# Two half-step feed-forwards: first sums copied out ahead of weight blocks, and the last stream turned by VectorE and a DRAM tile

## The chip, the core and the metric

The kernel runs on one core of a Trainium2 chip. The metric is the device time of one execution in microseconds (us); the median of three runs of the kernel before is 977.78 us (977.39 to 977.93). The core has five engines that run their own queues of instructions and wait for each other by semaphores: TensorE (PE in the profile; its weight loads are listed apart as PEld), VectorE (DVE), ScalarE (ACT), GpSimd (POOL) and SyncE (SP). SP, ACT and POOL issue DMAs here.

## The reference

Two consecutive layers of a decoder trunk on 256 tokens of 1024 features, everything in float32, batch 1, with 256 memory tokens and a feed-forward width of 2816:

```python
def rmsnorm(x, g):
    y = x32 * lax.rsqrt(jnp.mean(x32 * x32, axis=-1, keepdims=True) + EPS)
    return y.astype(x.dtype) * g

def swiglu(x, w_gate, w_up, w_down):
    return (jax.nn.silu(x @ w_gate) * (x @ w_up)) @ w_down
...
    mem_n = rmsnorm(mem, mem_norm)
    for l in range(DEPTH):
        x = x + 0.5 * swiglu(rmsnorm(x, ffn1_norm[l]), ffn1_w_gate[l], ffn1_w_up[l], ffn1_w_down[l])
        h = rmsnorm(x, mix_norm[l])
...
        x = x + memory_cross_attention(rmsnorm(x, xa_norm[l]), mem_n, xa_w_q[l], xa_w_kv[l], xa_w_o[l])
        x = x + 0.5 * swiglu(rmsnorm(x, ffn2_norm[l]), ffn2_w_gate[l], ffn2_w_up[l], ffn2_w_down[l])
    return rmsnorm(x, final_norm)
```

In layer 0 the cut lines add a mixer of a short convolution and sliding-window attention, in layer 1 one of block-sparse attention. Each layer so has two half-step feed-forwards, ffn1 ahead of the mixer and ffn2 behind the memory attention.

## The kernel before

**Layout.** The stream `x` lies with features on the 128 partitions and tokens along the free axis: 8 tiles of 128x256, one per 128 features. A product contracts over features, so no transposes stand between the steps. Only the end is other: the last down projection writes tokens on partitions, so that the output leaves in its own layout, and for this the stream has to be turned once into `xtok`, 2 tiles of 128 tokens by 1024 features (it lies in the buffer named `bias`). `to_tokens` does this on TensorE: 16 transposes of 128x128 against `ident` (L469) into four tiles `tr`, each copied out by ScalarE as 128x512 (L470). `evac_tok` adds the last sums to `xtok`.

**Float32 by parts.** A float32 operand is split in a high part (type fp32r) and the rest. A weight tile of 128x128 times an `x` tile takes two matmuls: `whi` against both parts of x (L378, 512 columns) and `wlo` against the high part (L379, 256 columns). The two halves of the accumulator `acc` are then put together by `join`: ScalarE copies the one out (L388), VectorE adds the other (L389). There are four `acc` tiles.

**The weight stream.** All weights come in one list of 128x128 tiles in the order of use. SP loads chunks of 16 tiles (1 MB, `raw<-in_w`), up to three ahead. `Stream` splits them by blocks of 8 tiles: ScalarE copies the block to `whi` (L128), VectorE subtracts to get `wlo` (L129), 128x1024 each, with five buffers of each. `take` hands out tiles and marks blocks up to four ahead as due; a due block is split when somebody calls `fill` or `flush`, or at the latest when a tile of it is needed. `fine` makes the blocks come in two halves. `pin`, when set, holds the pieces of a block to the order in which the program writes them; without it the scheduler may move them ahead of other work. `memory` (the memory attention) sets `pin` at its start and clears it at its end.

**A feed-forward.** `ffn` runs over 22 tiles of the hidden width; for each there is a group for gate and one for up, in two parts of four weight tiles: eight tiles, one block, one accumulator each. The products are taken of x times the norm's gain alone; the scale by the root mean square comes later. `squares` sums the squares of the tiles, `norm_scale` puts sums (L347), the power on GpSimd (L351) and the spread over partitions (L357) among the matmuls, and sets `n.ready`. Groups that end before that are joined, and their `evac` (scale, silu, product, split into `h`) waits in `n.waiting`. `evac` and the down projections flush due blocks.

**What sets the order.** `Order.run` writes the groups in sequence and tasks between them by an estimated time (`pe.after(delay, fn, cost)`). A scheduler then orders each engine's queue by estimated times, except what is kept in program order. The eight tiles `x` of a new norm come out of the preceding projection one by one, so at the start of ffn2 the first groups' matmuls stand interleaved: each new tile is used for the groups that are open.

Of the kernel before, what the change touches and what calls it, by code (L numbers as in the profile page):

```python
# [15 lines left out]
F32 = mybir.dt.float32  # L16
F32R = mybir.dt.float32r
AF = mybir.ActivationFunctionType
# [5 lines left out]
P = 128  # L24
D = 1024
KT = D // P
S = 256
# [196 lines left out]
def halves(t):  # L224

    return t.rearrange("p (b a) -> p b a", b=2)
# [17 lines left out]
def build(nc, tc, ctx, a):  # L244
    consts = ctx.enter_context(tc.tile_pool(name="consts", bufs=1))
    wpool = ctx.enter_context(tc.tile_pool(name="wpool", bufs=1))
    act = ctx.enter_context(tc.tile_pool(name="act", bufs=1))
    psum = ctx.enter_context(tc.tile_pool(name="psum", bufs=1, space=PSUM))
    dram = ctx.enter_context(tc.tile_pool(name="dram", bufs=1, space=DRAM))

    def acc_tile():
        return psum.tile([P, 512], F32, name="acc", bufs=4)
# [4 lines left out]
    def tr_tile():  # L257
        return psum.tile([P, 512], F32, name="tr", bufs=2)

    def w1():  # L260
        return act.tile([P, S], F32, name="w1", bufs=8)
# [8 lines left out]
    x = consts.tile([P, KT, S], F32, name="x")  # L270
# [3 lines left out]
    ws = Stream(nc, wpool, a["w0"], a["w"])  # L274
# [4 lines left out]
    ident = consts.tile([P, P], F32, name="ident")  # L279
# [8 lines left out]
    pt = tr_tile()  # L288
# [3 lines left out]
    pe = Order()  # L292
# [45 lines left out]
            nc.scalar.activation(sq, stream[:, k], AF.Square)  # L338
            nc.vector.tensor_tensor(n.acc, n.acc, sq, op=ALU.add)

    def norm_scale(n, delay=2300):


        def sums():
            pt = tr_tile()
            for t in range(2):
                nc.tensor.matmul(pt[:, t:t + 1], n.acc[:, t * P:(t + 1) * P], ones, start=True, stop=True)  # L347
            ms = act.tile([P, 2], F32, name="ms", bufs=2)
            nc.vector.tensor_scalar(ms, pt[:, :2], 1.0 / D, EPS, op0=ALU.mult, op1=ALU.add)
            n.rcol = act.tile([P, 2], F32, name="rcolm" if n.keep else "rcol", bufs=1 if n.keep else 2)  # L350
            nc.gpsimd.tensor_tensor(n.rcol, ms, mhalf, op=ALU.pow)  # L351
            pe.after(2200, spread, 120)

        def spread():
            pt = tr_tile()
            for t in range(2):
                nc.tensor.transpose(pt[:, t * P:(t + 1) * P], n.rcol[:, t:t + 1].to_broadcast([P, P]), ident)  # L357
            n.rbc = act.tile([P, S], F32, name="rbcm" if n.keep else "rbc", bufs=1 if n.keep else 2)
            nc.scalar.activation(n.rbc, pt[:, :S], AF.Copy)
            n.ready = True  # L360
            ws.fine = False
            for fn in n.waiting:
                fn()
            n.waiting = []

        pe.after(delay, sums, 250)

    def when_scaled(n, fn):
        if n.ready:
            fn()  # L370
        else:
            n.waiting.append(fn)


    def mm(ps, w, x2, start, stop):


        nc.tensor.matmul(ps, w[0], x2.both, start=start, stop=False)  # L378
        nc.tensor.matmul(ps[:, :S], w[1], x2.high, start=False, stop=stop)  # L379
# [7 lines left out]
    def join(out, ps):  # L387
        nc.scalar.activation(halves(out), unpaired(ps[:, S:]), AF.Copy)  # L388
        nc.vector.tensor_tensor(halves(out), unpaired(ps[:, :S]), halves(out), op=ALU.add)  # L389
        return out  # L390
# [62 lines left out]
    def split_tile(src):  # L453
        return split_into(h_tile(), src)
# [6 lines left out]
            nc.vector.tensor_tensor(lo, src, hi.bitcast(F32), op=ALU.subtract)  # L461

    def to_tokens(out):
        def go():
            for u in range(2):
                for c in range(2):
                    pt = tr_tile()
                    for k in range(4):
                        nc.tensor.transpose(pt[:, k * P:(k + 1) * P], x[:, 4 * c + k, u * P:(u + 1) * P], ident)  # L469
                    nc.scalar.activation(out[:, u, c * 512:(c + 1) * 512], pt, AF.Copy)  # L470
        return go


    def ffn(which, layer, n, nxt, first=False, last=False):
# [14 lines left out]
        def gate_up(f, part, ks):  # L489
            def go():  # L490
                if ks[0] == 0:
                    cur[f, part] = acc_tile()
                ps = cur[f, part]
                w = f"{which}_w_{'up' if part else 'gate'}"
                for k in ks:
                    mm(ps, ws.take(w, layer, k * P, f * P), n.x[k], k == 0, k == KT - 1)
                if ks[-1] == KT - 1:
                    cur[f, part] = join(w1(), ps)
                    if part == 1:
                        when_scaled(n, lambda: evac(f, cur[f, 0], cur[f, 1]))  # L500

            return always, go, len(ks) * 327

        def evac(f, g, u):

            nc.vector.tensor_tensor(g, g, n.rbc, op=ALU.mult)
            nc.scalar.activation(g, g, AF.Silu)
            ws.fill()
            nc.vector.tensor_tensor(u, g, u, op=ALU.mult)
            ws.fill()  # L510
            h[f] = split_tile(halves(u))
            ws.flush()
# [73 lines left out]

        if first:
            pe.after(12000, lambda: [squares(n, k, x) for k in range(KT)], 0)
        norm_scale(n, 18200 if first else 2300)
        parts = (range(4), range(4, KT))  # L590
        ups = [(always, gates, FIRST * 327)] if first else []
        ups += [gate_up(f, part, ks) for f in range(FT) for part in range(2) for ks in parts
# [1 line left out]
        if last:  # L594
            xtok = act.tile([P, 2, D], F32, name="bias", bufs=1)
            gfin = act.tile([P, D], F32, name="kT", bufs=1)
            src = a["final_norm"]
            nc.sync.dma_start(gfin, bass.AP(tensor=src.tensor, offset=src.offset, ap=[[0, P], [1, D]]))
            pe.after(20000, to_tokens(xtok), 2000)
        pe.run(ups + (down_tok() if last else [down(j) for j in range(KT)]))  # L600


# [420 lines left out]
    def memory(layer, n, nxt, k2):  # L1023
        o = [None] * 4
        v2 = act.tile([P, 2, 2, 512], F32R, name="bias", bufs=1)

        def scale():
            n.rs = small("rs")
            nc.vector.tensor_scalar(n.rs, n.rcol, 128 ** -0.5, None, op0=ALU.mult)

        def evac_q(h):
            def fn(t):
                at = slice(h * P, (h + 1) * P)
                attend_all(n, split_into(q2_tile(), t), k2[h], lambda u: (v2[:, 0, u, at], v2[:, 1, u, at]),
                           lambda: made.get((layer, h // 2), math.inf), collector(o, h))
                ws.step()
            return fn

        when_scaled(n, scale)
        norm_scale(n)  # L1040
        ws.pin = tc.keep_in_program_order
        f = [group("xa_w_q", layer, h * P, n, evac_q(h), scaled=False) for h in range(4)]
        v = [mem_v_group(layer, i, v2[:, 0], v2[:, 1]) for i in range(2)]
        pe.run(f[0] + f[1] + v[0] + f[2] + f[3] + v[1] + out_proj("xa_w_o", layer, o, nxt, (2, 3)))
        ws.pin = None


    xn = lambda key: new_normed(key, "x", KT)
    n = xn(("ffn1_norm", 0))
# [50 lines left out]
    n, nxt = nxt, xn(("xa_norm", 0))  # L1100
    even_mixer(n, nxt, bias, sinks, kv2_tiles(), mem_keys(0))
    n, nxt = nxt, xn(("ffn2_norm", 0))
    memory(0, n, nxt, keys[0])
    bias = load_bias(1)
    n, nxt = nxt, xn(("ffn1_norm", 1))
    ffn("ffn2", 0, n, nxt)
    n, nxt = nxt, xn(("mix_norm", 1))
    ffn("ffn1", 1, n, nxt)
    n, nxt = nxt, xn(("xa_norm", 1))
    odd_mixer(n, nxt, bias, mem_keys(1))  # L1110
    n, nxt = nxt, xn(("ffn2_norm", 1))
# [74 lines left out]
```

## Time and profile before

| what | us |
|---|---|
| median of three runs | 977.78 |
| the profiled execution | 977.58 |
| its span | 975.8 |

How to read it: a timeline row has the start within the span, the duration, the engine, line and operation, output<-inputs, shapes, and in brackets a wait and what ended it. A waits row has the waiting instruction, the engine and line that ended the wait, then the total, the count and the mean in us. A group row ends with the total busy time, the mean in ns and the idle time before. The buffers' numbers are left out in the profile. The rows themselves stand in the prediction, where they are used.

### The profile page before, as it was taken

How to read it: one execution, taken by the hardware profiler on the slowest of the kernel's cores; microseconds unless marked ns; L12 is line 12 of the kernel's file. 1: busy time of each engine (PE TensorE's matmuls, PEld its weight loads, DVE VectorE, ACT ScalarE, POOL GpSimd, SP SyncE). 2: the span in 40 equal slices, each digit the busy share in tenths (PEclk: the TensorE clock that was granted, in tenths of full speed). 3: DMA queues.
4: the chain of work that ended last, by engine and by line, in shares of the span. 5: the costliest groups of instructions: out<-in, count | busy, mean ns of one | idle time of the engine just before them, and what ended most of it. 6: DMA issues, size and time to landing. Idle time of an engine off the chain costs nothing.

```text
span 975.8 us, 16900 instructions
## 1 busy us (share of the span) xinstructions
PE 963.8 (99%) x6576; PEld 903.5 (93%) x6576; DVE 759.2 (78%) x1355; ACT 614.1 (63%) x1139; POOL 27.7 (3%) x42
## 2 busy tenths in 40 slices
PE   8999999999999999999999999999999999999997
PEld 7899999999999899999999999999999989999896
DVE  7988777798878888876778888677877788888663
ACT  7666655696667666665556666556775767666541
POOL 1100000001000000000000000000000000000010
PEclk9999999999999999999999999999999999999999
DMA  9797556555535555656556566565645346565631
GB/s 354 292 352 258 180 210 206 173 186 197 189 131 210 189 210 213 198 195 212 193 196 203 192 211 205 187 213 173 241 148 195 102 158 225 206 210 186 210 130 43
DMA packets 28496, 194.73 MB, mean 200 GB/s; under 512 B 3298, under 2 KB 3938, under 8 KB 5760
## 3 DMA queue, kind: packets, MB, share of 16 engines
q1 hardware_dynamic: 27072, 187.84, 55.5%
q0 software_dynamic: 912, 5.37, 1.5%
q8 instruction: 51, 0.84, 0.3%
q10 hardware_dynamic: 432, 0.44, 0.1%
q14 instruction: 29, 0.24, 0.1%
HBM read 192.57 MB, written 4.22 MB: 202 GB/s over the span
## 4 chain that ended last, share of the span: by engine, by line
PE 97%; DVE 1%; DMA 0%; issue 0%; ACT 0%; SPq 0%; POOLq 0%
PE acc L378 41%; PE acc L379 21%; PE acc L383 7%; PE acc L385 7%; PE acc L384 7%; PE acc L555 1%; PE acc L554 1%; PE acc L553 1%; PE acc L891 1%; PE acc L890 1%; PE acc L892 1%; DMA raw<-in_w 0%; PE sc L553 0%; PE sc L555 0%; PE sc L554 0%; PE tr L687 0%
## 5 line engine op out<-in xcount | busy, mean ns | idle before, releaser
L128 ACT ACTIVATE whi<-raw 128x1024 fp32r<-128x1024 f32 (+2 forms) x375 | 369.8, 990 | 286.1 <-PE acc L378 141.4
L129 DVE TENSOR_TENSOR wlo<-raw,whi 128x1024 fp32r<-128x1024 f32 (+2 forms) x375 | 427.4, 1142 | 154.8 <-ACT whi L128 145.3
L378 PE MATMUL acc<-x,whi 128*128 128x512 f32 x1392 | 457.5, 383 | 3.5 <-DVE w L389 2.6
L379 PE MATMUL acc<-x,wlo 128*128 128x256 f32 x1392 | 377.6, 273 | 0.6 <-DVE wlo L129 0.6
L378 PEld LDWEIGHTS acc<-x,whi 128*128 128x128 f32 x1392 | 262.2, 189 | 40.4 <-DVE w L389 2.8
L379 PEld LDWEIGHTS acc<-x,wlo 128*128 128x128 f32 x1392 | 267.2, 192 | 1.7 <-DVE wlo L129 0.9
L378 PE MATMUL acc<-h,whi 128*128 128x512 f32 x462 | 151.3, 382 | 0.0
L379 PE MATMUL acc<-h,wlo 128*128 128x256 f32 x462 | 125.5, 273 | 0.0
L378 PEld LDWEIGHTS acc<-h,whi 128*128 128x128 f32 x462 | 87.1, 189 | 12.0
L379 PEld LDWEIGHTS acc<-h,wlo 128*128 128x128 f32 x462 | 88.7, 192 | 0.2
L384 PE MATMUL acc<-h,whi 128*128 128x256 f32 x322 | 87.8, 276 | 0.0
L385 PE MATMUL acc<-h,wlo 128*128 128x256 f32 x322 | 87.7, 275 | 0.0
L383 PE MATMUL acc<-h,whi 128*128 128x256 f32 x322 | 86.5, 276 | 0.0
L384 PE MATMUL acc<-x,whi 128*128 128x256 f32 x304 | 84.1, 278 | 0.0
L385 PE MATMUL acc<-x,wlo 128*128 128x256 f32 x304 | 83.8, 278 | 0.0
L383 PE MATMUL acc<-x,whi 128*128 128x256 f32 x304 | 83.0, 277 | 0.0
L389 DVE TENSOR_TENSOR w<-acc,w 128x256 f32<-128x256 f32 x195 | 81.4, 418 | 0.3
L388 ACT ACTIVATE w<-acc 128x256 f32<-128x256 f32 x195 | 72.0, 370 | 5.4 <-PE acc L379 5.2
L384 PEld LDWEIGHTS acc<-h,whi 128*128 128x128 f32 x322 | 61.7, 192 | 0.1
L385 PEld LDWEIGHTS acc<-h,wlo 128*128 128x128 f32 x322 | 61.7, 192 | 0.1
L383 PEld LDWEIGHTS acc<-h,whi 128*128 128x128 f32 x322 | 60.6, 192 | 0.4 <-DVE x L441 0.2
L384 PEld LDWEIGHTS acc<-x,whi 128*128 128x128 f32 x304 | 58.2, 192 | 0.2
(205 smaller groups left out, 1159.7 us busy)
## 6 DMA issues: line engine op xcount, KB each, us to landing
raw<-in_w SPq DMA_DIRECT2D x171, 1024.0 KB, 4.9
dists<-line POOLq DMA_DIRECT2D x2, 1536.0 KB, 12.2
raw<-in_memT SPq DMA_DIRECT2D x3, 1024.0 KB, 5.1
raw<-in_w SPq DMA_DIRECT2D x6, 384.0 KB, 6.1
bias<-dists POOLq DMA_DIRECT2D x2, 1024.0 KB, 11.4
x<-in_xT SPq DMA_DIRECT2D x1, 1024.0 KB, 7.6
out<-bias SPq DMA_DIRECT2D x2, 320.0 KB, 2.4
kT<-in_final_norm SPq DMA_DIRECT2D x1, 512.0 KB, 5.3
```

The costliest lines, as they stand in the source:

```text
L128: for ins in (self.nc.scalar.activation(hi[:, at], src, AF.Copy), self.nc.vector.tensor_tensor(lo[:, at], src, hi[:, at].bitcast(F32), op= ...
L129: self.nc.vector.tensor_tensor(lo[:, at], src, hi[:, at].bitcast(F32), op=ALU.subtract)):
L378: nc.tensor.matmul(ps, w[0], x2.both, start=start, stop=False)
L379: nc.tensor.matmul(ps[:, :S], w[1], x2.high, start=False, stop=stop)
L383: nc.tensor.matmul(ps[:, :S], w[0], x2.high, start=start, stop=False)
L384: nc.tensor.matmul(ps[:, :S], w[0], x2.low, start=False, stop=False)
L385: nc.tensor.matmul(ps[:, :S], w[1], x2.high, start=False, stop=stop)
L388: nc.scalar.activation(halves(out), unpaired(ps[:, S:]), AF.Copy)
L389: nc.vector.tensor_tensor(halves(out), unpaired(ps[:, :S]), halves(out), op=ALU.add)
L553: nc.tensor.matmul(ps, hh, wh, start=f == 0, stop=False)
L554: nc.tensor.matmul(ps, hh, wl, start=False, stop=False)
L555: nc.tensor.matmul(ps, hl, wh, start=False, stop=f == FT - 1)
```

## The change

Three edits. First, in ffn1 and ffn2 `gate_up` flushes the due blocks behind each join as long as the norm's scale isn't ready. Second, `pin` is no longer cleared at the end of `memory` but by `norm_scale` of the feed-forward behind it, once its scale is ready. So at the start of ffn2 the blocks are split in the program's order behind the joins, whereas the scheduler placed them before. Third, `to_tokens` no longer uses TensorE. For each pair of x tiles VectorE transposes 128x512 in squares of 32x32 into a tile `q2` (two buffers); eight GpSimd DMAs of 32x8x32 (runs of 32 elements) write it to a DRAM tile `tok`, 32 DMAs in all; one more loads `tok` into `xtok`. It starts 6000 (the order's estimated ns) behind the norm's scale in place of 20000 behind the start of the feed-forward, and its transposes and stores are kept in program order.

```diff
-    def norm_scale(n, delay=2300):
+    def norm_scale(n, delay=2300, unpin=False):
...
             n.ready = True
             ws.fine = False
+            if unpin:
+                ws.pin = None
...
     def to_tokens(out):
-        def go():
-            for u in range(2):
-                for c in range(2):
-                    pt = tr_tile()
-                    for k in range(4):
-                        nc.tensor.transpose(pt[:, k * P:(k + 1) * P], x[:, 4 * c + k, u * P:(u + 1) * P], ident)
-                    nc.scalar.activation(out[:, u, c * 512:(c + 1) * 512], pt, AF.Copy)
-        return go
+        tok = dram.tile([S, D], F32, name="tok")
+        to = tok.rearrange("(c i) (k p j) -> p k i c j", i=32, p=4, j=32)
+        for k in range(0, KT, 2):
+            t = act.tile([P, 2 * S], F32, name="q2", bufs=2)
+            tc.keep_in_program_order(nc.vector.transpose(t, x[:, k:k + 2].rearrange("p k s -> p (k s)")))
+            for p in range(4):
+                for i in range(2):
+                    tc.keep_in_program_order(nc.gpsimd.dma_start(
+                        to[p, k + i], t[32 * p:32 * p + 32, i * S:(i + 1) * S].rearrange("i (c j) -> i c j", j=32)))
+        nc.gpsimd.dma_start(out, tok.rearrange("(u q) f -> q u f", u=2))
...
                     if part == 1:
                         when_scaled(n, lambda: evac(f, cur[f, 0], cur[f, 1]))
+                    if not n.ready:
+                        ws.flush()
...
-        norm_scale(n, 18200 if first else 2300)
+        norm_scale(n, 18200 if first else 2300, unpin=True)
...
-            pe.after(20000, to_tokens(xtok), 2000)
+            when_scaled(n, lambda: pe.after(6000, lambda: to_tokens(xtok), 0))
...
         pe.run(f[0] + f[1] + v[0] + f[2] + f[3] + v[1] + out_proj("xa_w_o", layer, o, nxt, (2, 3)))
-        ws.pin = None
```

Below are queue rows with the buffers' numbers, which name a tile through the program. Lines of the changed kernel are higher by 2 at the matmuls and joins (L378 to L389 are L380 to L391), by 8 in `evac`.

ScalarE's queue at the start of ffn2 in layer 0, before (`x_4022` is the last x tile of this norm; `acc_4030`, `acc_4059`, `acc_4098` are the sums of groups 0 to 2, `whi_4086` and `whi_4091` the blocks of groups 4 and 5):

```order
L128 ACTIVATE whi_4086<-raw_3940 128x1024
L317 ACTIVATE x_4022<-x_69,vecs_70 128x2x128
L338 ACTIVATE sq_4025<-x_69 128x256
L128 ACTIVATE whi_4091<-raw_3940 128x1024
L388 ACTIVATE w1_4049<-acc_4030 128x256
L128 ACTIVATE whi_4142<-raw_4031 128x1024
L388 ACTIVATE w1_4076<-acc_4059 128x256
L128 ACTIVATE whi_4147<-raw_4031 128x1024
L388 ACTIVATE w1_4117<-acc_4098 128x256
```

The same place of ScalarE's queue in the changed kernel (groups 0 to 2 are `acc_4030`, `acc_4063`, `acc_4098`; the blocks of groups 4 and 5 are `whi_4052` and `whi_4083`):

```order
L317 ACTIVATE x_4022<-x_69,vecs_70 128x2x128
L338 ACTIVATE sq_4025<-x_69 128x256
L390 ACTIVATE w1_4049<-acc_4030 128x256
L128 ACTIVATE whi_4052<-raw_3940 128x1024
L390 ACTIVATE w1_4080<-acc_4063 128x256
L128 ACTIVATE whi_4083<-raw_3940 128x1024
L128 ACTIVATE whi_4142<-raw_4031 128x1024
L128 ACTIVATE whi_4147<-raw_4031 128x1024
L390 ACTIVATE w1_4117<-acc_4098 128x256
```

The copy of group 0 stood behind group 5's block and now stands ahead of group 4's; group 4's block has moved from ahead of the last x tile to behind that copy. VectorE's queue moves likewise.

TensorE's queue at the same start, before, from the end of group 3's (`acc_4120`) thirteen matmuls on (`acc_4154` is group 4):

```order
L378 MATMUL acc_4120<-x_3998,whi_4004 128x512
L379 MATMUL acc_4120<-x_3998,wlo_4005 128x256
L378 MATMUL acc_4030<-x_4022,whi_3884 128x512
L379 MATMUL acc_4030<-x_4022,wlo_3885 128x256
L378 MATMUL acc_4059<-x_4022,whi_3909 128x512
L379 MATMUL acc_4059<-x_4022,wlo_3910 128x256
L378 MATMUL acc_4098<-x_4022,whi_3958 128x512
L379 MATMUL acc_4098<-x_4022,wlo_3959 128x256
L378 MATMUL acc_4120<-x_4022,whi_4004 128x512
L379 MATMUL acc_4120<-x_4022,wlo_4005 128x256
L347 MATMUL tr_4052<-ones_95,sqacc_3982 128x1 x2
L378 MATMUL acc_4154<-x_3904,whi_4086 128x512
```

And in the changed kernel, from group 2's pair on the tile before the last:

```order
L380 MATMUL acc_4098<-x_3998,whi_3958 128x512
L381 MATMUL acc_4098<-x_3998,wlo_3959 128x256
L380 MATMUL acc_4030<-x_4022,whi_3884 128x512
L381 MATMUL acc_4030<-x_4022,wlo_3885 128x256
L380 MATMUL acc_4063<-x_4022,whi_3909 128x512
L381 MATMUL acc_4063<-x_4022,wlo_3910 128x256
L380 MATMUL acc_4098<-x_4022,whi_3958 128x512
L381 MATMUL acc_4098<-x_4022,wlo_3959 128x256
L381 MATMUL acc_4120<-x_3904,wlo_4005 128x256
L380 MATMUL acc_4120<-x_3917,whi_4004 128x512
L381 MATMUL acc_4120<-x_3917,wlo_4005 128x256
```

The last pairs of groups 0 to 2 stood behind thirteen matmuls of group 3 and now stand ahead of them, right behind group 2's pair on the tile before.

VectorE's queue in ffn2 of layer 1 in the changed kernel, at the third and fourth of the new transposes (`q2` is the transposed tile, `raw`, `whi` and `wlo` belong to weight blocks, `acc` to a join, `h` to the hidden tiles):

```order
L391 TENSOR_TENSOR w1_9920<-acc_9901,w1_9920 128x256
L472 STREAM_TRANSPOSE q2_9666<-x_69 128x512
L449 TENSOR_TENSOR h_9898<-w1_9884,h_9898 128x2x128
L514 TENSOR_TENSOR w1_9920<-w1_9920,rbc_9570 128x256
L129 TENSOR_TENSOR wlo_10002<-raw_9902,whi_10001 128x1024
L391 TENSOR_TENSOR w1_9940<-acc_9923,w1_9940 128x256
L517 TENSOR_TENSOR w1_9940<-w1_9920,w1_9940 128x256
L129 TENSOR_TENSOR wlo_10007<-raw_9902,whi_10006 128x1024
L391 TENSOR_TENSOR w1_9976<-acc_9957,w1_9976 128x256
L449 TENSOR_TENSOR h_9954<-w1_9940,h_9954 128x2x128
L472 STREAM_TRANSPOSE q2_9676<-x_69 128x512
```

The first two transposes stand together in front of the third of three L449 further up in this queue; the four are new, and the rows between them are those of before. On GpSimd's queue the 32 stores and the load stand behind the last L351 and ahead of the end's operations.

## The prediction

> **What bounds the kernel.** I read the busy times first, then the chain of waits, then the waits of TensorE by what ended them.
>
> ```profile
> span 975.8 us, 16900 instructions
> PE 963.8 (99%) x6576; PEld 903.5 (93%) x6576; DVE 759.2 (78%) x1355; ACT 614.1 (63%) x1139; POOL 27.7 (3%) x42
> PE 97%; DVE 1%; DMA 0%; issue 0%; ACT 0%; SPq 0%; POOLq 0%
> PE acc L378 <- DVE w L389: 2.6, 2, 1.3
> PE acc L378 <- ACT whi L128: 0.6, 1, 0.6
> PE acc L379 <- DVE wlo L129: 0.6, 1, 0.6
> ```
>
> TensorE (PE) is busy for 963.8 of 975.8 us and carries 97% of the chain. A change gains only by taking instructions off PE or by closing one of its waits. The largest waits (total, count, mean) are two, 2.6 us together, for the VectorE (DVE) half of a join. So the question is where these two stand, and how much PE work the change removes. The profiled execution took 977.58 us, 1.78 around its span; the median of the runs shown is 977.78, 0.20 above it.
>
> ```profile
> 322.39 0.38 PE L379 MATMUL acc<-x,wlo 128*128 128x256 f32 x2
> ...
> 324.58 0.38 PE L378 MATMUL acc<-x,whi 128*128 128x512 f32 x1
> 324.79 0.27 PE L379 MATMUL acc<-x,wlo 128*128 128x256 f32 x1
> ...
> 325.89 0.50 PE L347 MATMUL tr<-ones,sqacc 128*128 128x1 f32 x4
> ...
> 327.70 0.48 PE L378 MATMUL acc<-x,whi 128*128 128x512 f32 x1 [1.31 <-DVE w L389]
> ```
>
> ```profile
> 804.56 0.48 PE L378 MATMUL acc<-x,whi 128*128 128x512 f32 x1 [1.31 <-DVE w L389]
> ```
>
> The timeline of PE (start, duration, instruction, wait in brackets) shows the start of the second feed-forward in layer 0, and the same wait in layer 1. Four accumulators exist; the fifth group, the row at 327.70, needs that of group 0. PE stopped at 327.70 − 1.31 = 326.39. Group 0 got its last pair of matmuls only at 324.58 and 324.79 and closed about 325.0, because 13 matmuls of group 3 stand ahead of it in PE's order.
>
> ```profile
> 324.99 1.06 ACT L128 ACTIVATE whi<-raw 128x1024 fp32r<-128x1024 f32 x1 [4.63 <-PE acc L378]
> 325.96 0.37 ACT L388 ACTIVATE w<-acc 128x256 f32<-128x256 f32 x1
> ```
>
> ```profile
> 320.97 0.48 DVE L318 SCALAR_TENSOR_TENSOR x<-x,vecs 128x256 fp32r<-128x256 f32 x1
> ...
> 326.08 1.23 DVE L129 TENSOR_TENSOR wlo<-raw,whi 128x1024 fp32r<-128x1024 f32 x1 [3.16 <-PE acc L379]
> 327.23 0.42 DVE L389 TENSOR_TENSOR w<-acc,w 128x256 f32<-128x256 f32 x1
> ```
>
> The timelines of ScalarE (ACT) and DVE tell the other half. ACT idled 4.63 us in front of a weight block whose buffer group 0 still held, then split it for 1.06 us, and only then copied group 0 out (0.37). DVE stood likewise: 1.23 us of wlo, then the add of the join. From group 0's close to the join's end at 327.65 pass 2.65 us, 2.29 of them a weight block.
>
> **The two gaps: minus 2.62 us.** In the changed order ACT has the last x tile, its square, join 0, then the blocks; PE has the three last-tile pairs of groups 0 to 2 ahead of group 3's remainder. PE finished group 2's previous pair with the first of the two L379 at 322.39, about 322.6. The last x tile was there at 320.97 + 0.48 = 321.45, and it moves ahead of a 1.23 us wlo on DVE and a 1.06 us whi on ACT, so it is no later.
>
> ```profile
> 859.68 0.38 PE L378 MATMUL acc<-x,whi 128*128 128x512 f32 x1
> ...
> 862.30 0.38 PE L378 MATMUL acc<-x,whi 128*128 128x512 f32 x1
> ```
>
> These two rows are eight pairs apart, one group of steady work: 2.62 us, 0.327 a pair. Group 0 therefore closes near 322.6 + 0.33 = 322.9, 2.1 us earlier than before. The ACT copy takes 0.37 and the DVE add 0.42: done about 323.9 with 0.1 per hand-over, 2.5 us ahead of 326.39.
>
> What is late next? The block of group 4, split ahead of the last x tile before, now stands behind join 0. Its whi runs about 323.4 to 324.4 (1.06), its wlo 324.4 to 325.7 (1.23 and a hand-over). PE wants whi at 326.39 and wlo 0.2 later: a margin of **0.7 to 1.0 us**. The block of group 5 follows join 1, ends near 327.2 and is wanted at 326.39 + 2.62 = 329.0. Joins 2 and 3, behind three blocks, come near 330.0 and 331.6 on DVE; wanted at 326.39 + 2 × 2.62 = 331.6 and 334.3. Each has over 1.5 us. So both gaps close, 2 × 1.31 = 2.62. Bounds: nothing gained (rival 1), and no more than the 2.62 that the rows hold.
>
> The same edits touch the start of the first feed-forward of layer 1, near 497 us, where blocks now come in two halves behind the joins.
>
> ```profile
> 328.00:500.00 172.00, 172.00 (x1075) 158.86 (x1074) 133.39 (x216) 104.68 (x179) 2.11 (x2) 1.00 0.59 202
> ```
>
> This window (length, then busy PE, weight loads, DVE, ACT, POOL, clock, DMA share, GB/s) covers that start. PE is busy all 172.00 us, so there is nothing to gain; join 0 would wait behind two halves, some 2.4 us, and has 4 us before PE asks. I put it at nothing.
>
> **The 16 transposes: minus 1.50 us.** They stand among layer 1's gate and up groups, in the PE queue.
>
> ```profile
> 807.50 0.60 PE L469 MATMUL tr<-ident,x 128*128 128x128 f32 x4
> 807.85 0.46 PE L378 MATMUL acc<-x,whi 128*128 128x512 f32 x1
> ...
> 815.79 1.04 PE L469 MATMUL tr<-ident,x 128*128 128x128 f32 x8
> 816.59 0.46 PE L378 MATMUL acc<-x,whi 128*128 128x512 f32 x1
> ...
> 820.82 0.60 PE L469 MATMUL tr<-ident,x 128*128 128x128 f32 x4
> 821.17 0.36 PE L379 MATMUL acc<-x,wlo 128*128 128x256 f32 x1
> ```
>
> From start to start of the next matmul they hold PE for 0.35, 0.80 and 0.35 us: 1.50. The four ACT copies of L470 go too; ACT is 63% busy and no wait of PE names them: nothing.
>
> **What replaces them: nothing on the path, as long as GpSimd issues at its usual pace.** Four DVE transposes of 128x512 arrive, then 32 DMAs of 32 KB and one of 1 MB, all issued by GpSimd (POOL). The trace has no DVE transpose; the nearest rows of that shape are:
>
> ```profile
> L332 DVE TENSOR_TENSOR w<-w,w 128x512 f32<-128x512 f32 x18 | 12.3, 684 | 0.1
> L567 DVE CUSTOM_DVE_ANT_0 w<-bias 128x512 f32<-128x512 f32 x2 | 2.5, 1230 | 0.0
> ```
>
> So 0.68 to 1.23 us each, 2.7 to 4.9 in all; I take 0.68, the row with eighteen instances. What hides them is DVE's 22% of idle time and the distance between a group's close and the use of its accumulator: 3 × 2.62 = 7.86 us, less 0.8 for the join, or **about 6.5 us of cover** with hand-overs. Below nothing is excluded for DVE and POOL work, since neither takes anything off PE.
>
> The danger is a wait. The tile that a transpose writes has two buffers, so transpose 3 waits on DVE until the eight DMAs of transpose 1 have landed, transpose 4 for those of transpose 2, and behind each queue the wlo blocks and joins that PE needs.
>
> ```profile
> 816.77 1.09 DVE L447 TENSOR_TENSOR h<-w,h 128x256 fp32r<-128x256 f32 x3
> ...
> 832.92 0.41 DVE L447 TENSOR_TENSOR h<-w,h 128x256 fp32r<-128x256 f32 x1
> ...
> 838.16 0.42 DVE L447 TENSOR_TENSOR h<-w,h 128x256 fp32r<-128x256 f32 x1
> ```
>
> ```profile
> 307.72 0.98 POOL L845 DMA_DIRECT2D bias<-dists  x1 [26.53 <-PE tr L706]
> 307.00:318.00 11.00, 11.00 (x92) 10.75 (x92) 10.52 (x24) 8.99 (x19) 0.98 (x1) 1.00 0.77 286
> L845 POOL DMA_DIRECT2D bias<-dists x2 | 1.9, 948 | 34.0 <-PE tr L706 26.5 <-PE acc L379 7.5
> line<-kT POOLq DMA_DIRECT2D x1, 24.0 KB, 2.4
> bias<-in_onehot POOLq DMA_DIRECT2D x1, 99.0 KB, 6.9
> raw<-in_w SPq DMA_DIRECT2D x171, 1024.0 KB, 4.9
> ```
>
> The first fence is DVE's timeline; the second has a row of POOL's, the window around it, a group row (busy, mean ns) and DMA rows (size, us to landing).
>
> By the order, transposes 1 and 2 come in the run of three at 816.77, transpose 1 ending near 818.1; transpose 3 just before 832.92, transpose 4 just after 838.16, near 838.6. An issue takes i = 0.95 (the mean of 948 ns, two rows), and landing 2.4 to 6.9 (24 and 99 KB), say 4.6. Eight issues have landed 818.1 + 7.6 + 4.6 = 830.3, ahead of 832.9. Sixteen: 818.1 + 15.2 + 4.6 = 837.9, ahead of 838.6; with 6.9 it is 840.2, a wait of 1.6 under 6.5 of cover. Cost nothing. The 1 MB back load is issued about 846 (transpose 4's eight issues) and is first used after 940; at 4.9 us for such a load it has ample room. The 8192 runs of 128 B share the queues with the weight loads, which land in 4.9 us, come in chunks used in 2 × 2.62 = 5.24 us, and are asked for three chunks ahead: nothing.
>
> **Sum:** 977.58 − 2.62 − 1.50 = 973.46 for the profiled execution; 0.20 above it, as the median stands: **973.7 us**, 0.42% less.
>
> **A rule that speaks against it.** The issue at 307.72 took 0.98 us in a window where DVE was busy for 10.52 of 11 us, so it was held by at most a small part of DVE's work. The Trainium skill, page "SBUF — State Buffer", section "SBUF: two separate sides" (its box on the "DVE blocks DMA" trap and what follows it), says that a DMA issued from GpSimd can't write its descriptors while VectorE holds the shared port in a two-port operation, and gives about 620 ns alone against 3100 beside one. By an estimate from that page, i would be 3.1, and by rival 2 below the loss 16 × 3.1 + 4.6 − 27 = 27 us, the time about 1001. By this rule the issue at 307.72 should have been stretched too; its 0.98 us agrees with the page only if the DVE operations beside it were of another kind.
>
> **Rivals.**
>
> 1. *The gap moves to the next in line.* Where group 4's block stands behind join 0, a delay of 0.7 to 1.0 us in any of four hand-overs opens PE's wait again, now for wlo in place of the join. If it stays as long as it was, only the transposes are gained: 977.78 − 1.50 = **976.3**, within 0.2%. In part: near 975. For it: the margin is the smallest of the sum, and one hand-over is enough. Against: it starts 2.1 us earlier than before.
>
> 2. *Issues on GpSimd stretch, and DVE stands still behind the third and fourth transpose.* The point from which this decides: the loss is 16i + 4.6 − 20.5 − 6.5, with 20.5 = 838.6 − 818.1. It is nothing up to i = 1.40 and eats the whole gain of 4.12 at i = 1.66.
>
> ```profile
> 280.50 0.69 POOL L351 TENSOR_TENSOR rcol<-ms,mhalf 128x2 f32<-128x2 f32 x1 [40.85 <-DVE ms L349]
> 327.80 1.61 POOL L351 TENSOR_TENSOR rcol<-ms,mhalf 128x2 f32<-128x2 f32 x1 [19.11 <-DVE ms L349]
> ```
>
> That POOL does stretch is in these rows: one operation, 0.69 and 1.61 us. By this ratio i = 0.95 × 2.33 = 2.2, and the loss 35.2 + 4.6 − 27 = 12.8: 973.7 + 12.8 = **986.5**, slower. Against: both DMA issues of that kind took about 0.95, and those here have a thirty-second of the bytes.
>
> That the edits don't reach the order can be left out: the rows of the changed order show join 0 ahead of the blocks.
>
> **Chances.** Forecast 0.66. Rival 1: 0.20, of which 0.14 within 0.2% (975.8 to 979.7, about what a measurement of this kernel tells from no change) and 0.06 short of it. Rival 2: 0.14, slower. Faster 0.66 + 0.06 = 0.72, same 0.14, slower 0.14. The range goes from 972.6 (the sum and 1 us for what two rows of 0.6 and the run-to-run spread hold) to 976.4 (rival 1 in full), leaving out 0.14 for rival 2 and a few hundredths below.
>
> **What would show it.** Right: no wait of over 0.3 us on PE near 326 and 803, no transposes of x on PE, DVE transposes of 0.6 to 1.2 us, POOL's issues about 0.95 apart, no DVE wait of over 6 us near 832 and 838. Wrong: a PE wait for L129 or L128 at the fifth group (rival 1), or a DVE wait at the third or fourth transpose with a PE wait for a join behind it (rival 2).

## The result and the profile after

| | before | changed |
|---|---|---|
| median, us | 977.86 (977.39 to 977.93, 6 runs) | 972.52 (972.07 to 973.35, 6 runs) |
| the profiled execution / its span, us | 977.58 / 975.8 | 972.72 / 970.9 |

The ratio of the changed kernel to before is 0.9947, with a 95% interval of 0.9934 to 0.996: between 3.9 and 6.5 us faster, 5.2 at the middle. The forecast was 973.7 with 972.6 to 976.4: the median is 1.2 us under the forecast and 0.1 under the low end of the range. By the ratio, 0.9947 of the 977.78 that the forecast starts from, it is 972.6, just on that end. One execution of e1, one of e2 and one of the kernel before beside e9 and e10 took 1685 to 3594 us and are left out of the medians and ratios below.

First the busy times of the changed kernel, the share of the chain, and the waits of TensorE (total, count and longest; the third number is not the mean, as it is called above):

```profile
PE 961.6 (99%) x6560; PEld 901.4 (93%) x6560; DVE 761.1 (78%) x1361; ACT 612.7 (63%) x1137; POOL 47.5 (5%) x75
PE 98%; DVE 1%; DMA 0%; ACT 0%; SPq 0%; issue 0%; POOLq 0%
PE tr L290 <- DVE warm L273: 1.1, 1, 1.1
PE acc L380 <- ACT whi L128: 1.0, 1, 1.0
PE acc L381 <- DVE wlo L129: 0.6, 1, 0.6
PE acc L380 <- DVE x L318: 0.3, 1, 0.3
```

The 2.6 us for the join are gone. What is left are waits in the first 24 us of the span.

The timelines of ScalarE and VectorE, at the place that the prediction showed of before (line numbers are 2 higher now):

```profile
323.47 0.38 ACT L390 ACTIVATE w<-acc 128x256 f32<-128x256 f32 x1 [2.33 <-PE acc L381]
323.75 1.05 ACT L128 ACTIVATE whi<-raw 128x1024 fp32r<-128x1024 f32 x1
...
323.88 0.42 DVE L391 TENSOR_TENSOR w<-acc,w 128x256 f32<-128x256 f32 x1 [1.79 <-ACT w L390]
324.83 1.23 DVE L129 TENSOR_TENSOR wlo<-raw,whi 128x1024 fp32r<-128x1024 f32 x1 [0.52 <-ACT whi L128]
```

ScalarE now waits for group 0's last matmul in front of the copy, not in front of a block. Join 0 ends at 324.30, the block of group 4 at 326.06.

To see where the time went, the same matmuls are set side by side: the timeline of TensorE before (first fence) and changed (second), in each the second matmul of group 4 in layer 0, that of group 4 in layer 1, and one just behind the last transposes.

```profile
328.02 0.27 PE L379 MATMUL acc<-x,wlo 128*128 128x256 f32 x1
...
804.88 0.27 PE L379 MATMUL acc<-x,wlo 128*128 128x256 f32 x1
...
821.37 0.38 PE L378 MATMUL acc<-x,whi 128*128 128x512 f32 x1
```

```profile
326.71 0.38 PE L380 MATMUL acc<-x,whi 128*128 128x512 f32 x1
326.93 0.27 PE L381 MATMUL acc<-x,wlo 128*128 128x256 f32 x1
...
802.32 0.27 PE L381 MATMUL acc<-x,wlo 128*128 128x256 f32 x1
...
817.06 0.38 PE L380 MATMUL acc<-x,whi 128*128 128x512 f32 x1
308.10 0.98 POOL L853 DMA_DIRECT2D bias<-dists  x1 [26.53 <-PE tr L714]
```

The last row (GpSimd's timeline) is the one that stood at 307.72 before; it is released by TensorE, so this execution was 0.38 us late ahead of the first gap (its wait for the first `whi` is 1.0 us, before 0.6). From there the shift goes to 326.93 − 328.02 = −1.09, 802.32 − 804.88 = −2.56 and 817.06 − 821.37 = −4.31. Steps: **1.47** for the first gap, **1.47** for the second, **1.75** for the transposes, 4.69 in all. It stays at that to the end of TensorE's work: from the start of the GpSimd row to the end of the last matmul the kernel before takes 661.35 us and the changed one 656.66. This stretch, called TensorE's part below, leaves out the start and the end of the span.

Both terms of the forecast came out larger than their rows. A bracket counts idle time from the end of the record in front, but in a full pipeline a matmul starts before that end (0.38 long, 0.22 apart). In front of group 4's first matmul at 327.70 stood the sums (L347) at 325.89. In the changed kernel the matmul behind the same sums, still one of group 3, does not wait:

```profile
325.28 0.50 PE L347 MATMUL tr<-ones,sqacc 128*128 128x1 f32 x4
325.65 0.46 PE L380 MATMUL acc<-x,whi 128*128 128x512 f32 x1
325.95 0.27 PE L381 MATMUL acc<-x,wlo 128*128 128x256 f32 x1
```

It starts 0.37 us after the first sum; before it was 327.70 − 325.89 = 1.81. So the wait held TensorE for 1.44 us where the bracket says 1.31. Most of what is left to 1.47 is the next start: 0.32 later behind the wait, 0.30 later behind the sums without one.

The transposes of one run start 0.11 us apart (the run of eight is 1.04 long, that of four 0.60), and sixteen times that is the 1.75. The prediction counted each run only to the start of the next matmul, which comes 0.03 us after the start of the last transpose, and so left out some 0.08 of each of the three runs.

Then the replacement, in the group rows and DMA rows of the changed kernel:

```profile
L472 DVE STREAM_TRANSPOSE q<-x 128x512 f32<-128x512 f32 x4 | 2.7, 699 | 0.0
L475 POOL DMA_DIRECT2D tok<-q x32 | 18.5, 584 | 17.9 <-DVE q L472 16.1 <-DVE w L514 1.0 <-DMA tok<-q 0.5
tok<-q POOLq DMA_DIRECT2D x32, 32.0 KB, 3.7
bias<-tok POOLq DMA_DIRECT2D x1, 1024.0 KB, 7.7
844.84 0.72 POOL L477 DMA_DIRECT2D bias<-tok  x1 [5.04 <-PE acc L381]
806.00:920.00 114.00, 114.00 (x679) 104.29 (x679) 93.58 (x156) 71.57 (x129) 19.18 (x33) 1.00 0.67 229
```

A transpose takes 0.70 us, a store 0.58 to issue and 3.7 to land, and in the window that holds all of it (806 to 920) TensorE is busy for all 114.00 us. VectorE had no idle time ahead of a transpose (the 0.0 of the first row).

The rest, 5.2 to 5.3 less 4.7, lies at the end. The last ScalarE DMA of the output, before and in the changed kernel:

```profile
971.66 0.35 ACTq L578 DMA_DIRECT2D out<-bias  x1
```

```profile
967.37 0.35 ACTq L586 DMA_DIRECT2D out<-bias  x1
```

From this issue to the end of the span it is 4.14 us before and 3.57 now (the trace has the spans as 975.803 and 970.942): **0.57 us** that no term of the forecast holds. The start of this execution was 0.38 late, so 4.69 + 0.57 − 0.38 = 4.88, against 4.86 between the spans.

### The profile page after: what moved, and what is told of

Same layout as the page of the kernel before. It is cut to its first block, busy times and chain, and to the rows that moved or that the text cites. A ratio compares the mean times of both kernels' runs of the same rounds, so it can differ in the third digit from the quotient of the medians.

```text
span 970.9 us, 16921 instructions
## 1 busy us (share of the span) xinstructions
PE 961.6 (99%) x6560; PEld 901.4 (93%) x6560; DVE 761.1 (78%) x1361; ACT 612.7 (63%) x1137; POOL 47.5 (5%) x75
## 3 DMA queue, kind: packets, MB, share of 16 engines
q1 hardware_dynamic: 27072, 187.84, 55.4%
q0 software_dynamic: 2208, 7.47, 2.2%
## 4 chain that ended last, share of the span: by engine, by line
PE 98%; DVE 1%; DMA 0%; ACT 0%; SPq 0%; issue 0%; POOLq 0%
PE acc L380 42%; PE acc L381 21%; PE acc L385 7%; PE acc L387 7%; PE acc L386 7%; PE acc L563 1%; PE acc L562 1%; PE acc L561 1%; PE acc L900 1%; PE acc L898 1%; PE acc L899 1%; PE sc L561 0%; PE sc L563 0%; PE sc L562 0%; DMA raw<-in_w 0%; PE tr L736 0%
## 5 line engine op out<-in xcount | busy, mean ns | idle before, releaser
L380 PE MATMUL acc<-x,whi 128*128 128x512 f32 x1392 | 457.2, 383 | 1.4 <-ACT whi L128 1.0
L380 PEld LDWEIGHTS acc<-x,whi 128*128 128x128 f32 x1392 | 262.1, 189 | 38.2 <-ACT whi L128 1.7
L380 PE MATMUL acc<-h,whi 128*128 128x512 f32 x462 | 151.3, 382 | 0.0
L380 PEld LDWEIGHTS acc<-h,whi 128*128 128x128 f32 x462 | 87.1, 189 | 12.0
L391 DVE TENSOR_TENSOR w<-acc,w 128x256 f32<-128x256 f32 x195 | 81.4, 418 | 3.9 <-ACT w L390 3.5
```

## The experiments

Two questions were open: which of the moves closes the gaps, and whether the 0.6 us at the end belong to the turning or to chance.

**e1, the order alone.** The flush and the longer pin; `to_tokens` and its start as before (the start, against the changed kernel):

```diff
-            when_scaled(n, lambda: pe.after(6000, lambda: to_tokens(xtok), 0))
+            pe.after(20000, to_tokens(xtok), 2000)
```

> The flush behind the joins and the longer pin alone; the stream is turned by TensorE as before. Theory A (the gain is what TensorE's queue saves: two gaps and the transposes, counted as the shift of TensorE's instructions against before, 1.47 us a gap and 1.74 us for the transposes): 2.94 us faster than before, about 974.9; no wait of TensorE for L391. Rival B (some 0.6 us more lie in the end of the kernel and belong to the turning): the same here, 974.9. By the prediction's terms 2.62 us, about 975.2.

Measured: 974.69 us, ratio 0.9967 (0.9954 to 0.998) to the 977.75 of before beside it: 2.0 to 4.5 us less. The trace is finer. TensorE's part is 658.41 us, 2.94 less than before, the 2 × 1.47 of the shifts, and no wait for the join is among TensorE's waits. The end takes 4.20 us, about as before. The 2.62 of the prediction was the right mechanism at a size a little too small.

**e2, the turning alone.** `to_tokens` and its start as in the changed kernel, everything else as before (the start, against before):

```diff
-            pe.after(20000, to_tokens(xtok), 2000)
+            when_scaled(n, lambda: pe.after(6000, lambda: to_tokens(xtok), 0))
```

> Only the turning by VectorE and DRAM; blocks and pin as before. Theory A: 1.74 us faster than before, about 976.1, with both waits of 1.3 us for the join's VectorE half still there; from the issue of the last output DMA to the end of the span 3.5 to 4.2 us as in either kernel. Rival B: 2.3 us or more faster, about 975.4, and always about 3.5 us at the end. By the prediction's term 1.50, about 976.3.

Measured: 975.39 us, ratio 0.9976 (0.9966 to 0.9985), 1.5 to 3.3 us less than before. TensorE's part is 659.60, 1.75 less. The waits hold the two gaps as they were:

```profile
PE acc L378 <- DVE w L389: 2.6, 2, 1.3
```

The end of this kernel:

```profile
span 973.4 us, 16918 instructions
969.86 0.35 ACTq L582 DMA_DIRECT2D out<-bias  x1
```

From this row to the end (973.424 in the trace) are 3.56 us, as in the changed kernel. So TensorE's parts add up (2.94 + 1.75 = 4.69), and the 0.6 come with the turning: rival B. In e1, without the turning, they are missing.

**e3, without the longer pin.** The flush and the turning stay:

```diff
-        norm_scale(n, 18200 if first else 2300, unpin=True)
+        norm_scale(n, 18200 if first else 2300)
...
         pe.run(f[0] + f[1] + v[0] + f[2] + f[3] + v[1] + out_proj("xa_w_o", layer, o, nxt, (2, 3)))
+        ws.pin = None
```

> The changed kernel with the pin cleared at the end of the memory attention as before; the flush and the turning stay. The queues at both starts stand as before (a block ahead of the last x tile, another ahead of the first copy, thirteen matmuls of group 3 ahead of group 0's last pair). Theory A: both gaps are back, 2.94 us slower than the changed kernel, about 1.74 faster than before (976.1). Rival: the flush alone is what helps, and the time is that of the changed kernel, about 972.7.

Measured: 975.4 us, ratio 0.9974 (0.9963 to 0.9984). In its waits both gaps are back:

```profile
PE acc L380 <- DVE w L391: 2.6, 2, 1.3
```

This is e2's time, and TensorE's part is 659.59, e2's too: without the pin the flush does nothing at these two places, since the scheduler moves the blocks ahead again. The kernel with the pin and no flush has the same order of ScalarE and TensorE there as before, so it was not run.

**e4, matmul order alone.** In the changed kernel the blocks of groups 4 and 5 are split ahead of join 0; TensorE's order stays:

```diff
                 if ks[-1] == KT - 1:
+                    if not n.ready and ws.pin and f == 0 and part == 0:
+                        ws._due_to(ws.n_due + 1)
+                        ws.flush()
                     cur[f, part] = join(w1(), ps)
```

> The changed kernel, but at both starts the blocks of groups 4 and 5 are written ahead of join 0, so that ScalarE and VectorE have join 0 behind them as before, while TensorE keeps the order of the changed kernel (group 0 closes some 2 us earlier). Theory A1 (both moves count: group 0's early close is worth some 2 us, the copy ahead of a block some 1.8): join 0 ends about 0.5 us after TensorE wants it, a wait of 0.3 to 0.5 us for L391 at each start, some 1 us slower than the changed kernel (973.6). Theory A2 (the copy ahead of weight blocks is all): waits of about 1.3 us are back at both, 2.9 us slower (975.5). Theory A3 (the matmul order is all): no wait, as the changed kernel.

Measured: 972.04 us, ratio 0.9944 (0.9932 to 0.9957), and TensorE has no wait for a join. The timeline of VectorE and then of TensorE:

```profile
324.58 1.23 DVE L129 TENSOR_TENSOR wlo<-raw,whi 128x1024 fp32r<-128x1024 f32 x1 [1.05 <-ACT whi L128]
325.72 0.42 DVE L391 TENSOR_TENSOR w<-acc,w 128x256 f32<-128x256 f32 x1
...
326.91 0.38 PE L380 MATMUL acc<-x,whi 128*128 128x512 f32 x1
```

Join 0 stands behind a block as before and ends at 326.14; group 4 begins at 326.91, without waiting, 0.77 us later. The expectation of 0.5 us of wait was wrong: it took the matmul behind the sums (L347) for the first of group 4, but in the changed order six matmuls of group 3 still follow the sums. The early close of group 0 alone closes the gaps.

**e5, the copy alone.** Joins 0 and 1 stand ahead of group 5's block, TensorE's order is that of before (the pin of e3, and then the lines below; `join` gives its third argument to its two instructions):

```diff
-                    cur[f, part] = join(w1(), ps)
+                    start = which == "ffn2" and f == 0 and part == 0
+                    cur[f, part] = join(w1(), ps, tc.keep_in_program_order if start else None)
...
                     if not n.ready:
                         ws.flush()
+                    if start:
+                        ws.pin = tc.keep_in_program_order
```

> The changed kernel with the other half of the move alone: at both starts ScalarE and VectorE have join 0 (and 1) ahead of group 5's block as in the changed kernel, while TensorE keeps the order of before (group 3's thirteen matmuls ahead of group 0's last pair, which closes at about 325.0) and group 4's block stands ahead of the last x tile. Theory B1 (each of the two moves is worth about 2 us against a gap of 1.47, so one is enough): join 0 ends at about 325.9, TensorE wants it at 326.4, no wait for L391, the time of the changed kernel (972.5). Theory B2 (the matmul order alone closes the gaps, as e4 would also have it): two waits of 1.3 us, about 975.4.

Measured: 972.29 us, ratio 0.9942 (0.993 to 0.9955), no wait for a join. The timelines of ScalarE, VectorE and TensorE:

```profile
324.86 0.66 ACT L390 ACTIVATE w<-acc 128x256 f32<-128x256 f32 x2 [4.80 <-PE acc L381]
...
325.27 0.75 DVE L391 TENSOR_TENSOR w<-acc,w 128x256 f32<-128x256 f32 x2 [2.67 <-ACT w L390]
...
325.94 0.46 PE L380 MATMUL acc<-x,whi 128*128 128x512 f32 x1
```

ScalarE waits 4.80 us for group 0, which closes as late as before, copies it and group 1 at once, and VectorE has added the first by about 325.7; TensorE starts group 4 at 325.94, right behind its sums. So either move alone is enough, as theory B1 said. TensorE's part is 656.66 us in the changed kernel, e4 and e5 alike. They differ in how long join 0 is done ahead of group 4: 2.4, 0.77 and some 0.25 us.

**e6 and e7, the end.** In the trace's records of the closing instructions GpSimd stood before for 0.39 us between two that the trace calls drain (to 974.97) and range clear of semaphores (from 975.36); in the changed kernel for 0.03. The turning adds 33 instructions to GpSimd's page count (42 to 75), and 39 to the trace's list of its queue, which has its waits too (72 to 111). e6 adds 39 memsets to the kernel before, e7 89 to the changed one (39 + 89 = 128), all early in the program (the diff of e6; 89 in e7):

```diff
+        if which == "ffn1" and layer == 1:
+            scr = act.tile([P, 2], F32, name="scr", bufs=1)
+            for _ in range(39):
+                nc.gpsimd.memset(scr, 0.0)
```

> The kernel before with 39 memsets of 128x2 added to GpSimd's queue in its first 10 us, where it is idle; nothing else. The end of the span, from the issue of the last output DMA to the end, took 4.17 us before and 3.57 in all kernels that turn on VectorE. Theory C1 (one instruction fetch for GpSimd falls on the closing instructions of the kernel before, and the 39 more instructions that the turning puts into GpSimd's queue move it away): the end takes 3.57 here too, about 0.6 us faster than before (977.15). Theory C2 (it comes from the turning itself, its DMAs or where xtok is written): 4.17, no difference.

> The changed kernel with 89 such memsets on GpSimd, which with the 39 added instructions of the turning make 128 (8 KB at 64 B each, the size of one instruction fetch), so that the fetch falls on the end again as before. Theory C1: the end takes about 4.17 us, 0.6 us slower than the changed kernel (973.1). Theory C2: 3.57, no difference from 972.5.

Measured: e6 977.24 us, ratio 0.9994 (0.9985 to 1.0002); e7 972.94, ratio 0.995 (0.9936 to 0.9963). The times alone can't tell, 0.4 to 0.6 us are within the intervals. The profiles can, e6 first, then e7:

```profile
span 975.1 us, 16939 instructions
971.34 0.35 ACTq L578 DMA_DIRECT2D out<-bias  x1
```

```profile
span 971.2 us, 17009 instructions
967.19 0.35 ACTq L586 DMA_DIRECT2D out<-bias  x1
```

The end shrinks from 4.14 to 3.79 in e6 and grows from 3.57 to 4.02 in e7 (the spans are 975.132 and 971.213 in the trace). In e6 GpSimd's clear follows its drain by 0.03 us; in e7 a stop of 0.34 us is back, one instruction further on (between the clear, to 970.46, and the next drain, from 970.80, which takes 0.18 us in place of 0.05). In the trace's list the stop stands ahead of the 69th of GpSimd's 72 instructions before and in e1, and ahead of the 197th of 199 in e7, 128 further on. In the nine other kernels neither place comes after the last wait for the output, and none of them has such a stop there. So the stop goes with a place in GpSimd's queue, and not with the turning itself; 0.34 us of the 0.57 left with it in e6.

That it is a fetch of instructions, as theory C1 has it, is not shown. The trace lists packets of instructions (8 and 16 KB), but none lies in any of the three stops, and the last one ahead of the stop before (973.89 to 974.20) has its like in e6 (from 973.57), where no stop follows.

**e9, the rest of the end.** In e6 SP still stood for 0.50 us between two closing instructions, in the changed kernel for 0.27. e9 is e6 with four small DMAs on SP:

```diff
+            spare = dram.tile([P, 2], F32, name="spare")
+            when_scaled(n, lambda: [nc.sync.dma_start(spare, n.rcol) for _ in range(4)])
```

> The kernel e6 (before with 39 memsets on GpSimd) and, on SP, four more DMAs of 1 KB to a spare DRAM tile at the middle of the program. In e6 the wait of GpSimd ahead of its closing clear of semaphores was gone (0.39 us before), but SP still stood for 0.5 us between two of its closing instructions, 0.3 in all kernels that turn on VectorE. Theory C1b (this is an instruction fetch too, SP's): the four DMAs and their semaphores move it away, and the end of the span shrinks from e6's 3.79 us to about 3.6; in time 0.2 us below e6, about 977.05. Theory C2b (it comes from the turning or from the output DMAs): 3.79 stays.

Measured: 977.55 us, ratio 1.0 (0.9991 to 1.001). The stop on SP became 0.40 us, not 0.27, and the end takes 4.01 us. Theory C1b isn't borne out.

The trace says what SP stood for. The instruction behind the stop waits for the semaphore that the last output DMA, ScalarE's, raises when it has landed. From this DMA's issue to that instruction pass 2.84 us before, 2.88 in e1, 2.85 in e6 and 2.81 in e9, but 2.61 to 2.66 in all eight kernels that turn on VectorE. So the other part of the 0.57 us, some 0.23, is a DMA that lands sooner, in kind what theory C2b says. The end of e9 is longer than that of e6 because on SP five short waits follow the one for this landing, in e6 only one.

Why it lands sooner stays open. In the four kernels where it lands late, an 8 KB packet of instructions starts with the last packets of this output (973.89 before); in the eight others none starts between its issue and its landing. No run shows that this packet is the cause.

**e8 and e10, the stores.** e8 gives the 32 stores to SP:

```diff
-                    tc.keep_in_program_order(nc.gpsimd.dma_start(
+                    tc.keep_in_program_order(nc.sync.dma_start(
```

> The changed kernel with the 32 stores to DRAM issued by SP in place of GpSimd; in SP's queue they stand in one piece among the weight loads. Theory D1 (a store that waits for its transpose holds back every weight load behind it; SP is held from the first transpose, about 815, to the fourth, about 834, and chunks are asked for only some 15 us ahead): TensorE waits for whi or wlo for 5 to 10 us between 830 and 845, 978 to 983. Theory D2 (loads are far enough ahead): no wait, 972.5; and if the descriptors of GpSimd's DMAs cost anything, a few tenths faster.

Measured: 972.73 us in a single run, with no such wait. The timeline of SP:

```profile
797.12 16.68 SPq L103 DMA_DIRECT2D raw<-in_w  x5
815.09 16.77 SPq L475 DMA_DIRECT2D tok<-q  x32
831.96 64.79 SPq L103 DMA_DIRECT2D raw<-in_w  x16
```

For 17 us no weight load was issued, and TensorE didn't wait: the loads are further ahead than theory D1 allowed. The stores take 16.77 / 32 = 0.52 us each on SP against 0.58 on GpSimd, and they land after 1.7 us (the median of 32) against 3.7. Either queue will do here.

e10 cuts each store in four:

```diff
+                    for e in range(0, 32, 8):
+                        tc.keep_in_program_order(nc.gpsimd.dma_start(
+                            to[p, k + i, e:e + 8],
+                            t[32 * p + e:32 * p + e + 8, i * S:(i + 1) * S].rearrange("i (c j) -> i c j", j=32)))
```

> The changed kernel with each store to DRAM cut in four (8 of the 32 rows each; 128 stores of 8 KB). The scheduler puts the third and fourth transpose further back in VectorE's queue for it. Theory E1 (an issue costs about 0.58 us whatever its size): GpSimd issues for about 74 us, the load of xtok goes out near 890 and lands well before 937; no VectorE wait of over 2 us, the time of the changed kernel (972.5). Theory E2 (the cost goes with the number of runs): 0.15 us each, 19 us in all; the same time. Rival 2 of the prediction (VectorE stands behind the third or fourth transpose, TensorE waits for a join): 975 to 988.

Measured: 972.31 us, ratio 0.9946 (0.9931 to 0.996). The group row:

```profile
L476 POOL DMA_DIRECT2D tok<-q x128 | 71.1, 563 | 30.1 <-DVE q L472 12.0 <-DMA tok<-q 9.9 <-DVE w L519 8.1
908.08 0.74 POOL L479 DMA_DIRECT2D bias<-tok  x1 [3.68 <-ACT whi L128]
```

An issue costs 0.56 us for 8 KB and 0.58 for 32 KB: theory E1. GpSimd issues for 71.1 us, and the load of `xtok`, now at 908.08, is still in time; it is free because the scheduler puts transposes 3 and 4 later in VectorE's queue. How long VectorE may stand before TensorE feels it (the 6.5 us of the prediction) was therefore not tried: the scheduler avoids such a wait.

All kernels side by side, in us: TensorE's part, then the end of the span from the issue of the last output DMA, what passes of it until SP goes on behind this DMA's landing, and GpSimd's stop.

| kernel | TensorE's part | end | landing | stop |
|---|---|---|---|---|
| before | 661.35 | 4.14 | 2.84 | 0.39 |
| e1, order alone | 658.41 | 4.20 | 2.88 | 0.40 |
| e2, turning alone | 659.60 | 3.56 | 2.61 | none |
| e3, no longer pin | 659.59 | 3.56 | 2.61 | none |
| changed | 656.66 | 3.57 | 2.61 | none |
| e4, e5 | 656.66 | 3.57, 3.56 | 2.62, 2.61 | none |
| e6, before with 39 memsets | 661.35 | 3.79 | 2.85 | none |
| e7, changed with 89 memsets | 656.66 | 4.02 | 2.62 | 0.34 |
| e8, stores by SP | 656.66 | 3.68 | 2.61 | none |
| e9, e6 and DMAs on SP | 661.34 | 4.01 | 2.81 | none |
| e10, quarter stores | 656.67 | 3.61 | 2.66 | none |

In e8 a closing drain of ScalarE came 0.35 us late, and some 0.1 us of that shows in its end.

## Why the prediction was right, step by step

- **The two gaps.** Right: they closed, and e1 holds them alone. Mis-sized: 2.62 in the sum, 2.94 measured, because the bracket of a wait leaves out the overlap of the records (0.13 of the 0.16 us a gap). The bound "no more than the 2.62 that the rows hold" therefore did not hold.
- **How they closed.** The times of the new order came as worked out: group 0's copy began at 323.47, with the start of this execution 0.38 late 323.1 (about 322.9 for the close in the prediction); join 0 ended 2.4 us ahead of group 4 at 326.71 (2.5 forecast), wlo of group 4 at 326.06, 0.87 us ahead of the matmul that needs it at 326.93 (0.7 to 1.0 forecast). What the prediction didn't say is that either of the two moves was enough. It took the gap's 2.65 us between close and join as one piece with the late close; e4 and e5 show that each alone is larger than the gap.
- **First feed-forward of layer 1: nothing.** Right. TensorE is busy all through the window that covers it:

```profile
328.00:500.00 172.00, 172.00 (x1075) 158.85 (x1074) 134.33 (x219) 104.88 (x181) 1.31 (x2) 1.00 0.59 204
```

- **The 16 transposes.** Right in kind, 1.50 forecast, 1.75 measured: each of three runs was counted 0.08 too short.
- **What replaces them: nothing on the path.** Right, with more room than forecast: issue 0.58 in place of 0.95, landing 3.7 in place of 4.6. The stores don't share a queue with the weight loads, as the prediction has it: the profile counts GpSimd's packets on q0, 2208 against 912 before, and SP's on q1, 27072 in both. The price of an issue was taken from two DMAs of 1 MB; the timeline of GpSimd before has a write of 24 KB, nearer in size and in price:

```profile
42.11 0.64 POOL L836 DMA_DIRECT2D line<-kT  x1 [11.51 <-DVE kT L835]
```

- **The rule that speaks against it** did not show in the issues. The Trainium skill, "SBUF — State Buffer", section "SBUF: two separate sides", has a GpSimd DMA take some 3100 ns beside a two-port VectorE operation; 32 issues took 584 ns on average in a stretch where VectorE was busy for 93.58 of 114.00 us, and SP, which by that page is free of the lock, took 0.52 us. The page's figure is of a whole DMA; the prediction set it against the issue. The landing, 3.7 us from GpSimd and 1.7 from SP, leaves open whether something held GpSimd's stores behind their issue. Which of VectorE's operations here count as two-port, no run shows.
- **Rival 1** (the gap moves to the next in line): no; the margin held. **Rival 2** (GpSimd's issues stretch): no; i was 0.58, against the 1.40 from which it would have cost. **The rival that wasn't seen** lies outside the middle of the kernel: 0.57 us at the end, of instructions that no part of the diff touches. The step that failed is the sum, which changed TensorE's part alone ("a change gains only by taking instructions off PE or by closing one of its waits") and left the end of the span as it was. The three shortfalls, 0.32, 0.25 and 0.57, all point the same way and use up the 1.1 us that the range left below the forecast. Some 0.3 of the 0.57 is luck: it hangs on how many instructions GpSimd's queue happens to hold, and with 89 memsets more (e7) it was gone.

The sum as it should have stood: 2.94 + 1.75 + 0.57 = 5.26, against 5.2 to 5.3 measured.

## What to carry to other kernels

Size a wait by the shift of the same instruction in two traces, or add to its bracket what the records overlap (1.31 was worth 1.47 here); for instructions taken off a full engine, multiply their number by the distance of their starts within a run (16 × 0.11). When a wait has two causes in a row (a late close and a block ahead of the copy), work out each alone: if each exceeds the gap, half of the change would do, and the rest is margin. A flag that steers a scheduler must be tried without its partner (the flush without the pin did nothing), and instructions added to an idle queue may move a stop at the very end. For small effects compare one stretch of the traces between two fixed instructions: here it repeats to 0.01 us, where the medians carry more than 1 us of uncertainty.

## What the runs showed of the hardware that was not expected

- The end of a span depends on how many instructions GpSimd's queue holds: a stop of 0.39 us in its closing instructions went with 39 more of them (e6), and one of 0.34 came with 89 more than in the changed kernel (e7). The two stand 128 places apart in the queue.
- The last output DMA, 192 KB, landed 0.2 us sooner in the eight kernels that turn the stream on VectorE (2.61 to 2.66 us until SP goes on, against 2.81 to 2.88).
- The issue of a DMA to DRAM costs GpSimd 0.56 to 0.58 us whether it writes 8 KB or 32 KB in runs of 128 bytes; both sizes land in 3.7 us. From SP a store of 32 KB costs 0.52 and lands in 1.7.
- The first product behind the sums is followed 0.30 us later in place of 0.22 (325.65 and 325.95 in the changed kernel), without any wait.
